# Chunk attention's probabilities turned by VectorE and GpSimd's transfers instead of TensorE

## The chip, the core and the metric

The kernel runs on one core of one Trainium2 chip. A core has engines that run side by side, each through its own instructions in order: TensorE (PE in the profile; PEld is its loading of weights) multiplies matrices and writes PSUM, VectorE (DVE) and ScalarE (ACT) work on elements, GpSimd (POOL) here fills small buffers and issues some transfers, SyncE (SP) issues nearly all transfers (DMAs). All transfers run on the core's 16 DMA engines. Engines wait for one another by semaphores. SBUF is the on-chip memory of 128 partitions, PSUM the accumulators, device memory (DRAM) holds inputs and outputs.

The metric is the device time of one execution in microseconds (us). Three runs of the kernel before took 925.45, 925.61 and 925.86 us.

## What is computed

Two layers of one mixer each, for 256 positions of width 2048. One input projection feeds three groups of heads: A, softmax attention in chunks of 64 (8 heads of 128); B, gated linear attention (4 heads); M, cross-attention into 256 memory tokens (4 heads). Each group's output is gated by a SiLU path, the groups are joined, mapped by an output projection, added to the input and normalized. Group A is where the change lies. Cut to it:

```python
def chunk_band_attention(q, k, v, rel_table):
    ...
    scores = jnp.einsum('bnqhd,bnkhd->bhnqk', qc, k_band).astype(jnp.float32) * (Dh ** -0.5)
    ...
    bias = rel_table[:, rel_idx].astype(jnp.float32)
    scores = jnp.where(valid[None, :, None, None, :], scores + bias[None, None], NEG_INF)
    p = jax.nn.softmax(scores, axis=-1).astype(v.dtype)
    out = jnp.einsum('bhnqk,bnkhd->bnqhd', p, v_band)
    return out.reshape(B, S, H, Dh)

def hybrid_layer(x, mem, w_in, rel_table, gate_w, gate_b, gla_norm_g, w_mem_kv, w_out, ln_g, ln_b):
    h = x @ w_in
    ...
    y = jnp.concatenate([y_a * jax.nn.silu(a_z), y_b * jax.nn.silu(b_z), y_m * jax.nn.silu(m_z)], axis=-1)
    out = y @ w_out
    return layer_norm(DEEPNORM_ALPHA * x + out, ln_g, ln_b)
```

With 256 positions and a band of nine chunks, a position sees its own chunk and all before it.

## The kernel before

**Weights.** Every projection is computed from pieces of weights, mostly of 512 KB, each read once. SP loads a piece into a raw buffer (`piece`, L128); ScalarE casts it to the high half (L116), VectorE subtracts to get the low half (L117), and TensorE multiplies with both halves. The pool `wp` has four buffers each for raw, high and low. `ws_half` (L240) and `as_group` (L272) run one output group, piece by piece, and call `tick` after each piece: with a share of 1 after a piece of 512 columns, of 388/512 after one of 388 columns.

**Work between the pieces.** The heads are written as generators. `tick` (L52) advances a counter by the share and runs one step of one generator that is due; a `yield n` puts off the generator's next step until the counter is n further. At most two generators are active at a time; the others wait in a list. `finish` calls `tick` until given generators are done. So a head's matmuls stand between the matmuls of two pieces in TensorE's order.

**Order.** TensorE and SP run in program order (`manual_schedule`, L49). The instructions of VectorE, ScalarE and GpSimd are put in order by a planner that simulates the program; on the chip each engine then keeps that order. Weight loads stand in SP's order where the pieces stand in the program, and SP runs ahead of TensorE as far as buffers are free.

**A head of group A** (`a_head`, L503, 8 per layer). It issues the bias load of head h + 2 on SP (`load_bias`, L820; the loads of heads 0 and 1 stand ahead of all), multiplies queries and keys into PSUM (scores for two tiles of 128 queries: 128 and 256 keys, 384 columns), adds the bias on VectorE (L511), takes the maximum (L516), the exponential and its sum on ScalarE (L518), and normalizes (L519, L521). Three steps of the counter later TensorE transposes the probabilities in three blocks of 128x128 into PSUM (L526) and ScalarE copies them to SBUF (L528); two steps later TensorE multiplies them with the values (L532, L533) and ScalarE copies the result out (L534). The bias tiles have four buffers, used in turn.

**Around it.** Per layer the generators run in this order: `gla` (group B, L311) from the third group of values on, heads 0 to 3 once the second group of keys is done (after piece 24, counted from that group of values), heads 4 to 7 after piece 48, then four heads of group M (`m_head`). The group of values has eight pieces of 388 columns; the groups of queries, keys and gates have eight pieces of 512 KB or the like. Scratch tiles come from a pool of eight buffers used in turn (`scratch`, L98), PSUM banks from one of four (`bank`, L95).

Of the kernel before, what the change touches and what calls it, by code (L numbers as in the profile page):

```python
# [8 lines left out]
F32 = mybir.dt.float32  # L9
# [4 lines left out]
ALU = mybir.AluOpType  # L14
# [4 lines left out]
P = 128  # L19
# [3 lines left out]
CH = 64  # L23
# [13 lines left out]
def hybrid_trunk_kernel(  # L37
# [7 lines left out]
    pe, dve, act, pool, sp = nc.tensor, nc.vector, nc.scalar, nc.gpsimd, nc.sync  # L45
# [4 lines left out]
    waiting, active, done, now = [], [], set(), [0]  # L50

    def tick(share=1.0):  # L52

        now[0] += share
        while True:
            while waiting and len(active) < 2:
                active.append((waiting.pop(0), 0))
            due = [e for e in active if e[1] <= now[0]]
            if not due:
                return  # L60
            active.remove(due[0])
            g = due[0][0]
            after = next(g, None)
            if after is not None:
                active.append((g, now[0] + after))
                return
            done.add(g)

    def finish(gens):
        while not all(g in done for g in gens):  # L70
            tick()

    def enter(name, bufs=1, **kw):
        return ctx.enter_context(tc.tile_pool(name=name, bufs=bufs, **kw))

    cst = enter("cst")
    per = enter("per")
    opp = enter("opp", 5)
    wp = enter("wp", 4)
    hd = enter("hd", 1)  # L80
    sc = enter("sc", 8)
    sm = enter("sm", 1)
    psd = enter("psd", 2, space=bass.MemoryType.PSUM)
    psa = enter("psa", 4, space=bass.MemoryType.PSUM)

    uid = [0]

    def nm(s):
        uid[0] += 1
        return f"{s}_{uid[0]}"  # L90

    def mm(o, l, r, start, stop):
        pe.matmul(o, l, r, start=start, stop=stop, skip_group_check=True)  # L93

    def bank():  # L95
        return psa.tile([P, 512], F32, name=nm("bk"), tag="bk")

    def scratch(shape, dtype=F32):  # L98
        return sc.tile(shape, dtype, name=nm("sc"), tag="sc")

    def small(shape, tag, bufs=1):
        return sm.tile(shape, F32, name=nm(tag), tag=tag, bufs=bufs)

    ident = cst.tile([P, P], F32, name="ident")
    lmask = cst.tile([P, 6, CH], U8, name="lmask")
    eye = cst.tile([P, CH], F32, name="eye")
    eps = cst.tile([P, 2], F32, name="eps")

    def operand():
# [130 lines left out]
    def ws_half(src, xq):  # L240

        acc = psd.tile([P, 2, 2, T], F32, name=nm("acc"), tag="acc")
        for pc in range(4):
            wh, wl = piece(src[pc], 256, 4)
            xh, _, both = xq[pc]
            for j in range(4):
                for b in range(2):
                    mm(acc[:, b].rearrange("p h t -> p (h t)"), wh[:, j, b * P:(b + 1) * P], both[:, j], pc == j == 0, False)
                for b in range(2):
                    mm(acc[:, b, 1], wl[:, j, b * P:(b + 1) * P], xh[:, j], False, pc == j == 3)  # L250
            tick()
        return acc
# [58 lines left out]
    def gla(gw, gb, ng, gq, gk, lr, asv, yraw):  # L311
# [15 lines left out]

        def keep(lev, pb):

            for par in range(2):  # L330
                pv = pb[par].rearrange("p (g c) -> p g c", c=CH)
                if lev < 0:
                    dve.tensor_tensor(pairs[par], pv, eye.unsqueeze(1).to_broadcast([P, 4, CH]), op=ALU.mult)
                else:
                    dve.copy_predicated(pairs[par], lmask[:, lev].unsqueeze(1).to_broadcast([P, 4, CH]), pv)


        pt = bank()
# [51 lines left out]
        pt = bank()  # L390
# [8 lines left out]
        for c in range(3):  # L399
            rs = slice((c % 2) * 64, (c % 2) * 64 + 64)  # L400
            t = c // 2
            for b in range(2):
                for par in range(2):
                    h = 2 * b + par
# [9 lines left out]
        for c in range(3):  # L414
            t = c // 2
            src = kv[c % 2].rearrange("p (g c) -> p g c", c=P)[:, t * 2:t * 2 + 2]
            if c == 0:
                dve.tensor_copy(st[:, 0], src)
            else:
                for b in range(2):  # L420
                    dve.scalar_tensor_tensor(st[:, c, b], st[:, c - 1, b], elast[:, b * 4 + c:b * 4 + c + 1],
                                             src[:, b], op0=ALU.mult, op1=ALU.add)
        keep(-1, diagonal)
        keep(0, first)

        for levels in ((1, 2, 3), (4, 5)):
            nxt = [decayed(LEVELS[lev]) for lev in levels]
            yield 6
            pb = [[bank() for _ in range(2)] for _ in levels[::2]]
            halves = [[p[:, i % 2 * 256:i % 2 * 256 + 256] for p in pb[i // 2]] for i in range(len(levels))]  # L430
            for kq, half in zip(nxt, halves):
                products(*kq, half)
            for lev, half in zip(levels, halves):
                keep(lev, half)
# [7 lines left out]
        po = [bank() for _ in range(2)]  # L442
        far = [bank() for _ in range(2)]
        at = [slice(i * CH, (i + 1) * CH) for i in range(2)]
        for t in range(2):
            for b in range(2):
                g = t * 2 + b
                for half in range(2):
                    for par in range(2):
                        h = 2 * b + par  # L450
                        mm(po[half][at[par], g * P:(g + 1) * P], pairs[par][at[half], g],
                           asv[at[half], t, 16 + h * P:16 + (h + 1) * P], g == 0, False)
        for odd, even in ((1, 2), (3, None)):
            for b in range(2):
                for c in (odd, even):
                    if c is not None:
                        for par in range(2):
                            g = (c // 2) * 2 + b
# [28 lines left out]
    def gla_turned(yraw, ng, y):  # L487

        for par in range(2):
# [8 lines left out]
            dve.scalar_tensor_tensor(lo, ptv, ng[:, 0:1], hi.bitcast(F32), op0=ALU.mult, op1=ALU.subtract)  # L498
            yield 1

    SCALE = P ** -0.5

    def a_head(h, load_bias, bias, q, k, asv, y):  # L503

        if h + 2 < 8:
            load_bias(h + 2)
        pb = bank()
        mm(pb[:, 0:128], q[:, 0:128], k[:, 0:128], True, True)
        mm(pb[:, 128:384], q[:, 128:256], k, True, True)
        s = scratch([P, 384])  # L510
        dve.scalar_tensor_tensor(s, pb[:, :384], SCALE, bias[h], op0=ALU.mult, op1=ALU.add)  # L511
        mx = small([P, 2], "mx", 4)
        zs = small([P, 2], "zs", 4)
        own = (slice(0, 128), slice(128, 384))
        for t in range(2):
            dve.tensor_reduce(mx[:, t:t + 1], s[:, own[t]], AX.X, ALU.max, negate=True)  # L516
        for t in range(2):
            act.activation(s[:, own[t]], s[:, own[t]], AF.Exp, bias=mx[:, t:t + 1], accum_out=zs[:, t:t + 1])  # L518
        dve.reciprocal(zs, zs)  # L519
        for t in range(2):  # L520
            dve.tensor_scalar(s[:, own[t]], s[:, own[t]], zs[:, t:t + 1], None, op0=ALU.mult)  # L521
        yield 3

        pt = bank()
        for i in range(3):
            pe.transpose(pt[:, i * P:(i + 1) * P], s[:, i * P:(i + 1) * P], ident)  # L526
        pT = scratch([P, 384])
        act.copy(pT, pt[:, :384])  # L528
        yield 2
        po = bank()  # L530
        v0 = 528 + h * P
        mm(po[:, 0:256], asv[:, 0, v0:v0 + P], pT[:, 0:256], True, False)  # L532
        mm(po[:, 128:256], asv[:, 1, v0:v0 + P], pT[:, 256:384], False, True)  # L533
        act.copy(y, po[:, :256])  # L534
        yield 2

    def m_head(h, q, mk, mv, y):
# [11 lines left out]
        dve.tensor_reduce(mx, pb.rearrange("p (t m) -> p t m", t=2), AX.X, ALU.max, negate=True)  # L549
        dve.tensor_scalar(mx, mx, SCALE, None, op0=ALU.mult)  # L550
        s = scratch([P, 2, 256])
        for t in range(2):
            act.activation(s[:, t], pb[:, t * 256:(t + 1) * 256], AF.Exp, bias=mx[:, t:t + 1], scale=SCALE, accum_out=zs[:, t:t + 1])
        dve.reciprocal(zs, zs)
# [59 lines left out]
    def wo_pieces(l, n):  # L614

        if n < 3:
            return [w512[l, G_WO + n, pc] for pc in range(8)]
        return [[w256[l, i, pc // 2][:, pc % 2 * 512:pc % 2 * 512 + 512] for i in range(2)] for pc in range(8)]
# [141 lines left out]
    for l in range(L):  # L760
# [27 lines left out]
        if l == 0:  # L788
            sp.dma_start(ident, ident_d)
            lm = wp.tile([P, 6, CH], I32, name="lm", tag="raw")  # L790
            sp.dma_start(lm, lmask_d)
            dve.tensor_copy(lmask, lm)
            dve.tensor_tensor(eye, ident[:, :CH], ident[:, CH:], op=ALU.add)

        asv = per.tile([P, 2, 1552], F32, name=nm("asv"), tag="asv")

# [21 lines left out]
        bias = {}  # L818

        def load_bias(h):  # L820
            bias[h] = hd.tile([P, 384], F32, name=nm("bias"), tag="bias", bufs=4)
            sp.dma_start(bias[h], relw[l, h])

        load_bias(0)
        load_bias(1)
        if l > 0:
# [4 lines left out]
        for half in range(2):  # L831
            values(2 + half)
            q = heads(G_AQ0 if half == 0 else G_AQ1)
            k = heads(G_AK0 if half == 0 else G_AK1)
            gens.append([a_head(half * 4 + h, load_bias, bias, q[:, h], k[:, h], asv, yraw[1 + half][:, h]) for h in range(4)])
            waiting.extend(gens[-1])
# [36 lines left out]
        for n in range(WO_N):  # L873
            if last:
                g, b = scratch([P, 512]), scratch([P, 512])
            else:
                both = per.tile([P, 2, 512], F32, name=nm("gb"), tag=f"yr{n}")
                g, b = both[:, 0], both[:, 1]
# [3 lines left out]
            src = wo_pieces(l, n)  # L882
# [122 lines left out]
```

## Time and profile before

| | before |
|---|---|
| median of three runs | 925.61 us (925.45 to 925.86) |
| the profiled execution | 925.59 us |
| its span, first to last instruction | 923.8 us |
| TensorE busy | 916.7 us, 5500 matmuls |
| VectorE busy | 587.9 us, 812 instructions |
| ScalarE busy | 498.2 us, 714 |
| GpSimd busy | 21.8 us, 49 |
| TensorE's mean granted clock | 0.998 |
| moved by DMA | 178.85 MB, mean 194 GB/s |

How to read the rows in what follows. A row of a group of instructions reads: line of the kernel, engine, operation, output <- inputs by name, shapes, count | busy us, mean ns of one | idle us of the engine just before them <- what ended it. A row in order of time reads: start us, us, engine, line, operation, tensors, count [idle before <- releaser]. A row of waits reads: waiting engine and line <- releaser and its line: us in total, times, longest. A row of DMA issues reads: tensors, queue, count, KB each, median us from the issue to the landing. A row of stretches reads: from:to, length, then busy time and count of TensorE, weight load, VectorE, ScalarE, GpSimd, then granted clock, share of the DMA engines, GB/s. Names: `bk` is a PSUM bank, `acc` a projection's accumulator, `sc` a scratch tile, `wh` and `wl` the halves of a piece, `asv` the values, `qk` queries and keys.

### The profile page before, as it was taken

The numbers are of one execution on the slowest core, as the hardware profiler recorded it, in microseconds if no ns is written. First come the engines' busy times: TensorE is split into PE (matmuls) and PEld (weight loads), VectorE is DVE, ScalarE is ACT, GpSimd is POOL, SyncE is SP. The second block draws the span as 40 slices with busy tenths as digits, with TensorE's granted clock in tenths as the row PEclk, the third lists the DMA queues.
The fourth block names the chain that finished last, engine by engine and source line by source line (L and its number), as shares of the span: only waits on it lengthen the run. The fifth ranks groups of instructions, "written<-read, shape, count | busy, mean of one in ns | idle before, by whom it ended". The sixth has DMA issues, their size and how long they took to land.

```text
span 923.8 us, 14249 instructions
## 1 busy us (share of the span) xinstructions
PE 916.7 (99%) x5500; PEld 806.5 (87%) x5500; DVE 587.9 (64%) x812; ACT 498.2 (54%) x714; POOL 21.8 (2%) x49
## 2 busy tenths in 40 slices
PE   9999999999999999999999999999999999999997
PEld 7889998998888888888888899889888888888885
DVE  6764478665564666555587666975655555766566
ACT  6644485484454675433566445754744555754350
POOL 1000000000000000000000000000000000110000
PEclk9999999999999999999999999999999999999999
DMA  9955865546554566756675466546555544667652
GB/s 306 334 189 174 306 207 173 161 165 194 183 162 160 171 206 200 219 193 196 227 249 164 150 205 204 193 154 196 170 193 166 164 152 160 199 222 223 198 163 92
DMA packets 71253, 178.85 MB, mean 194 GB/s; under 512 B 7304, under 2 KB 31240, under 8 KB 70928
## 3 DMA queue, kind: packets, MB, share of 16 engines
q1 hardware_dynamic: 69120, 173.30, 57.1%
q0 software_dynamic: 1920, 4.36, 1.8%
q8 instruction: 43, 0.70, 0.3%
q10 hardware_dynamic: 144, 0.26, 0.1%
q14 instruction: 26, 0.21, 0.1%
HBM read 175.77 MB, written 2.10 MB: 193 GB/s over the span
## 4 chain that ended last, share of the span: by engine, by line
PE 98%; DMA 0%; DVE 0%; ACT 0%; SPq 0%; issue 0%
PE acc L93 89%; PE bk L93 8%; PE bk L526 1%; DMA raw<-w 0%; PE bk L561 0%; PE bk L590 0%; PE bk L494 0%; PE bk L393 0%; SPq L177 0%; ACT res L746 0%; ACT wh L116 0%; DVE stats L731 0%; PE bk L340 0%; DVE res L730 0%; DVE res L682 0%
## 5 line engine op out<-in xcount | busy, mean ns | idle before, releaser
L117 DVE TENSOR_TENSOR wl<-raw,wh 128x1024 fp32r<-128x1024 f32 (+3 forms) x321 | 370.0, 1154 | 255.9 <-ACT wh L116 254.9
L116 ACT CAST wh<-raw 128x1024 fp32r<-128x1024 f32 (+3 forms) x321 | 318.7, 994 | 329.9 <-PE acc L93 236.5
L93 PE MATMUL acc<-x,wh 128*128 128x512 f32 x1248 | 398.0, 400 | 0.1
L93 PE MATMUL acc<-wh,x 128*128 128x512 f32 (+2 forms) x1236 | 357.3, 370 | 0.1
L93 PEld LDWEIGHTS acc<-x,wl 128*128 128x128 f32 x1248 | 234.4, 188 | 55.3
L93 PEld LDWEIGHTS acc<-wh,x 128*128 128x128 f32 x1236 | 227.0, 188 | 27.9 <-ACT wh L116 0.6
L93 PE MATMUL acc<-x,wl 128*128 128x256 f32 x1248 | 246.0, 278 | 0.0
L93 PE MATMUL acc<-wl,x 128*128 128x512 f32 (+2 forms) x618 | 228.0, 369 | 0.0
L93 PEld LDWEIGHTS acc<-x,wh 128*128 128x128 f32 x1248 | 192.0, 189 | 1.9 <-ACT wh L116 0.4
L93 PEld LDWEIGHTS acc<-wl,x 128*128 128x128 f32 x618 | 116.0, 188 | 15.0 <-DVE wl L117 0.9
L518 ACT ACTIVATE sc<-sc,mx 128x128 f32<-128x128 f32 (+1 forms) x32 | 14.4, 450 | 20.3 <-DVE mx L516 20.3
L511 DVE SCALAR_TENSOR_TENSOR sc<-bk,bias 128x384 f32<-128x384 f32 x16 | 8.9, 554 | 12.7 <-PE bk L93 12.7
L382 ACT ACTIVATE sc<-sc 128x512 f32<-128x512 f32 x12 | 7.6, 633 | 12.5 <-DVE sc L380 12.5
L117 DVE TENSOR_TENSOR x<-sc,x 128x512 fp32r<-128x512 f32 x20 | 13.3, 684 | 0.7 <-ACT x L116 0.7
L116 ACT CAST x<-raw 128x1024 fp32r<-128x1024 f32 x5 | 5.3, 1053 | 15.3 <-DMA raw<-memT 12.7
L117 DVE TENSOR_TENSOR x<-res,x 128x512 fp32r<-128x512 f32 (+2 forms) x14 | 10.5, 765 | 4.2 <-ACT x L116 4.1
L93 PE MATMUL bk<-qk,qk 128*128 128x128 f32 (+1 forms) x64 | 13.1, 326 | 0.0
L117 DVE TENSOR_TENSOR x<-raw,x 128x1024 fp32r<-128x1024 f32 x5 | 6.1, 1225 | 10.9 <-ACT x L116 10.9
L93 PE MATMUL bk<-sc,asv 128*128 128x256 f32 (+1 forms) x64 | 13.0, 326 | 0.0
L262 DVE SCALAR_TENSOR_TENSOR sc<-acc,sc 128x512 f32<-128x512 f32 x19 | 12.9, 681 | 0.0
L116 ACT CAST x<-sc 128x512 fp32r<-128x512 f32 x20 | 11.8, 615 | 1.3 <-DVE sc L598 1.3
L623 DVE SCALAR_TENSOR_TENSOR res<-res,acc 128x512 f32<-128x512 f32 x15 | 9.7, 684 | 4.2 <-PE acc L93 4.2
(209 smaller groups left out, 567.8 us busy)
## 6 DMA issues: line engine op xcount, KB each, us to landing
raw<-w SPq DMA_DIRECT2D x214, 512.0 KB, 3.9
raw<-w SPq DMA_DIRECT2D x64, 388.0 KB, 3.3
raw<-w SPq DMA_DIRECT2D x83, 256.0 KB, 3.2
bias<-relw SPq DMA_DIRECT2D x16, 192.0 KB, 4.1
res<-xT SPq DMA_DIRECT2D x4, 512.0 KB, 5.0
res<-xn SPq DMA_DIRECT2D x1, 2048.0 KB, 8.2
raw<-memT SPq DMA_DIRECT2D x4, 512.0 KB, 4.3
res<-memT SPq DMA_DIRECT2D x6, 256.0 KB, 6.1
```

What stands on the lines that cost most here:

```text
L93: pe.matmul(o, l, r, start=start, stop=stop, skip_group_check=True)
L116: act.copy(hi, src)
L117: dve.tensor_tensor(lo, src, hi.bitcast(F32), op=ALU.subtract)
L262: dve.scalar_tensor_tensor(dst, a, scale, dst, op0=ALU.mult, op1=ALU.add)
L382: act.activation(dd, dd, AF.Abs)
L511: dve.scalar_tensor_tensor(s, pb[:, :384], SCALE, bias[h], op0=ALU.mult, op1=ALU.add)
L518: act.activation(s[:, own[t]], s[:, own[t]], AF.Exp, bias=mx[:, t:t + 1], accum_out=zs[:, t:t + 1])
L526: pe.transpose(pt[:, i * P:(i + 1) * P], s[:, i * P:(i + 1) * P], ident)
L623: dve.scalar_tensor_tensor(r, r, ALPHA, acc, op0=ALU.mult, op1=ALU.add)
```

## The change

The three transposes on TensorE and the copy by ScalarE leave the head. In their place `turned` lets VectorE transpose the probabilities in blocks of 32x32 into a scratch tile, GpSimd issue four transfers of 32 partitions each into a tile in device memory (each writes 128 rows of 96 floats), and GpSimd issue one transfer that reads that tile back into `pT`, 128 partitions of 384 floats. `pT` and the tile in device memory have three buffers each of their own. The two yields of 3 and 2 between scores and values become one of 7. Three generators may be active instead of two. The bias tiles have three buffers instead of four. The tile `eye` is no longer kept: each layer makes it in a scratch tile.

```diff
-            while waiting and len(active) < 2:
+            while waiting and len(active) < 3:
                 active.append((waiting.pop(0), 0))
...
+    tp = enter("tp", 3)
...
+    drm = enter("drm", 3, space=bass.MemoryType.DRAM)
...
-    eye = cst.tile([P, CH], F32, name="eye")
...
         def keep(lev, pb):
 
+            if lev < 0:
+                eye = scratch([P, CH])
+                dve.tensor_tensor(eye, ident[:, :CH], ident[:, CH:], op=ALU.add)
...
+    def turned(dst, src, n):
+
+        blocks = scratch([P, 4, n])
+        dve.transpose(blocks.rearrange("p b (g j) -> p g b j", j=32), src.rearrange("p (g b j) -> p g b j", b=4, j=32))
+        home = drm.tile([P, 4, n], F32, name=nm("home"), tag=f"home{n}")
+        for a in range(4):
+            pool.dma_start(home[:, a].rearrange("(b i) n -> i b n", b=4), blocks[a * 32:(a + 1) * 32])
+        pool.dma_start(dst, home)
...
             dve.tensor_scalar(s[:, own[t]], s[:, own[t]], zs[:, t:t + 1], None, op0=ALU.mult)
-        yield 3
-
-        pt = bank()
-        for i in range(3):
-            pe.transpose(pt[:, i * P:(i + 1) * P], s[:, i * P:(i + 1) * P], ident)
-        pT = scratch([P, 384])
-        act.copy(pT, pt[:, :384])
-        yield 2
+        pT = tp.tile([P, 4, 96], F32, name=nm("pT"), tag="pT")
+        turned(pT, s, 96)
+        yield 7
         po = bank()
         v0 = 528 + h * P
-        mm(po[:, 0:256], asv[:, 0, v0:v0 + P], pT[:, 0:256], True, False)
-        mm(po[:, 128:256], asv[:, 1, v0:v0 + P], pT[:, 256:384], False, True)
+        pv, pov = pT.rearrange("p a (g j) -> p g a j", j=32), po[:, :256].rearrange("p (t a j) -> p t a j", t=2, j=32)
+        mm(pov, asv[:, 0, v0:v0 + P], pv[:, 0:2], True, False)
+        mm(pov[:, 1], asv[:, 1, v0:v0 + P], pv[:, 2], False, True)
         act.copy(y, po[:, :256])
...
-            dve.tensor_tensor(eye, ident[:, :CH], ident[:, CH:], op=ALU.add)
...
         def load_bias(h):
-            bias[h] = hd.tile([P, 384], F32, name=nm("bias"), tag="bias", bufs=4)
+            bias[h] = hd.tile([P, 384], F32, name=nm("bias"), tag="bias", bufs=3)
             sp.dma_start(bias[h], relw[l, h])
```

## The prediction

> **What bounds the kernel now.** I read the page from the top, then the waits of TensorE and of the DMA queue on SP, then the instructions in order of time around the heads of chunk attention.
>
> ```profile
> span 923.8 us, 14249 instructions
> PE 916.7 (99%) x5500; PEld 806.5 (87%) x5500; DVE 587.9 (64%) x812; ACT 498.2 (54%) x714; POOL 21.8 (2%) x49
> PE 98%; DMA 0%; DVE 0%; ACT 0%; SPq 0%; issue 0%
> ...
> PE bk L93 <- DVE eps L759: 1.1, 1, 1.1
> ```
>
> TensorE is busy 99% of the span, it is 98% of the chain that ended last, and its longest wait is 1.1 us, at the start. So any work taken from TensorE shortens the run, and any moment in which it lacks an operand lengthens it. The profiled execution took 925.59 us: 923.8 of span and 1.8 around it; the median of the runs is 925.61. I work from 925.6.
>
> What keeps TensorE fed is SP, whose queue is in program order and runs ahead:
>
> ```profile
> SPq L141 <- DVE wl L117: 516.3, 232, 5.4
> SPq L822 <- DVE sc L511: 5.0, 2, 2.8
> ...
> 198.34 0.56 DVE L511 SCALAR_TENSOR_TENSOR sc<-bk,bias 128x384 f32<-128x384 f32 x1 [1.98 <-PE bk L93]
> 198.93 0.33 SPq L822 DMA_DIRECT2D bias<-relw  x1
> ...
> 229.28 0.43 SPq L822 DMA_DIRECT2D bias<-relw  x1
> ```
>
> SP normally waits for a raw buffer (L141 on the subtraction L117). Twice it waited at L822, the load of a head's bias, for L511, which reads an older bias: L511 ended at 198.34 + 0.56 = 198.90 and the load left at 198.93. With four bias buffers that cost 2.8 us of lead at most. The load at 229.28 stands in the code just after head 5 starts, and head 5's score product ran at 250.49 (next fence): SP leads TensorE by 21 us.
>
> **The change, part by part.** First the prices of TensorE's pieces of work:
>
> ```profile
> 174.85 0.82 PE L93 MATMUL bk<-qk,qk 128*128 128x128 f32 x4
> 177.71 1.16 PE L93 MATMUL bk<-sc,sc 64*64 64x64 f32 x64
> 185.26 0.49 PE L526 MATMUL bk<-ident,sc 128*128 128x128 f32 x3
> ...
> 235.25 0.81 PE L93 MATMUL bk<-sc,asv 128*128 128x256 f32 x4
> 247.05 0.82 PE L93 MATMUL bk<-qk,qk 128*128 128x128 f32 x4
> 250.49 0.82 PE L93 MATMUL bk<-qk,qk 128*128 128x128 f32 x4
> 256.72 0.49 PE L526 MATMUL bk<-ident,sc 128*128 128x128 f32 x3
> 259.87 0.49 PE L526 MATMUL bk<-ident,sc 128*128 128x128 f32 x3
> 263.00 0.81 PE L93 MATMUL bk<-sc,asv 128*128 128x256 f32 x4
> 266.45 0.81 PE L93 MATMUL bk<-sc,asv 128*128 128x256 f32 x4
> ```
>
> These are heads 4 and 5 of layer 0 (and head 0 above); between two neighbours lies one weight piece, two where the code has two. With p a piece, q the scores, t the transposes, v the values: p+q = 3.44, 2p+q = 6.23, p+t = 3.15, p+v = 3.45, so p = 2.79, q = 0.65, t = 0.36, v = 0.66; check: 235.25 to 247.05 is 4p+v = 11.8. A piece of 388 columns is 177.71 - 174.85 - q = 2.21, and the recurrence's step at 177.71 costs 185.26 - 177.71 - 3 x 2.21 = 0.92.
>
> (1) *Transposes removed from TensorE.* The row of the group is 48 matmuls; their price by spacing is t per head, between 0.24 (only the three starts) and 0.36. I take 0.34: 16 x 0.34 = **-5.4 us**. The value products keep their sizes and stay at v.
>
> (2) *Order of steps.* With three active and yields of 7 and 2, I followed the counter of `tick` by hand. The same count for the kernel before gives the order seen in the trace (head 0 after piece 25, counted from the third group of values, heads 4 and 5 after 49 and 50). After the change: scores of heads 0 to 7 after pieces 25, 27, 33, 37, 49, 50, 51, 59; values after 34, 36, 40, 44, 56, 57, 58, 66. No `finish` has to idle.
>
> (3) *Three bias buffers.* Now the load for head h+2 waits for head h-1's L511, and head h may start one piece after head h-1. Load 7 (in head 5, after piece 50) needs head 4's L511 (after piece 49); load 3 (after 27) needs head 0's (after 25). SP, 21 us ahead, stops there, with every later weight piece behind it. Prices:
>
> ```profile
> L511 DVE SCALAR_TENSOR_TENSOR sc<-bk,bias 128x384 f32<-128x384 f32 x16 | 8.9, 554 | 12.7 <-PE bk L93 12.7
> L117 DVE TENSOR_TENSOR wl<-raw,wh 128x1024 fp32r<-128x1024 f32 x248 | 302.5, 1222 | 192.8 <-ACT wh L116 192.3
> L116 ACT CAST wh<-raw 128x1024 fp32r<-128x1024 f32 x248 | 259.6, 1049 | 244.6 <-PE acc L93 161.8 <-issue 68.2 <-DMA raw<-w 4.7
> L117 DVE TENSOR_TENSOR wl<-raw,wh 128x776 fp32r<-128x776 f32 x64 | 61.8, 966 | 60.1 <-ACT wh L116 59.9
> L116 ACT CAST wh<-raw 128x776 fp32r<-128x776 f32 x64 | 53.9, 843 | 82.3 <-PE acc L93 74.7 <-issue 4.0 <-DMA raw<-w 3.4
> ...
> raw<-w SPq DMA_DIRECT2D x214, 512.0 KB, 3.9
> raw<-w SPq DMA_DIRECT2D x64, 388.0 KB, 3.3
> raw<-w SPq DMA_DIRECT2D x2, 128.0 KB, 2.8
> ```
>
> At load 7, from the start of head 4's scores: L511 ends at 0.86 + 0.56 = 1.42 (its row at 247.91, below), the bias issue takes 0.43, then piece 51 leaves at 1.88, lands 3.9 later, is cast in 1.05 and subtracted in 1.22: high half at 6.9, low half at 8.15 with 0.05 per handover. TensorE gets to piece 51 at q + p + q = 4.09. It waits 2.8, does two matmuls (0.47), then waits 0.8 for the low half: 3.6, and 0.3 more as half a reduction of another head may stand ahead on VectorE: 3.9. Bounds: a landing of 2.8 (the 128 KB row) gives 2.8; a whole subtraction ahead gives 5.1. Two layers: **+7.8 us**.
>
> At load 3: high half at 1.88 + 3.3 + 0.05 + 0.84 = 6.1, low half at 7.1; TensorE arrives at q + 2.21 + 0.92 + 2.21 + q = 6.64 and needs the low half at about 7.0. 0 to 1.2 us, taken 0.5: two layers **+1.0 us**. Loads 4 and 5 find four to six pieces between, over 11 us, and hold nobody. After each hold SP refills four raw buffers at once.
>
> (4) *The turn itself.* It replaces a PSUM copy on ScalarE by a VectorE transpose and five transfers of GpSimd, and must end within the time to the values.
>
> ```profile
> 247.91 0.56 DVE L511 SCALAR_TENSOR_TENSOR sc<-bk,bias 128x384 f32<-128x384 f32 x1 [0.77 <-PE bk L93]
> 251.05 0.55 DVE L521 TENSOR_SCALAR sc<-sc,zs 128x128 f32<-128x128 f32 x2
> 256.36 0.55 DVE L521 TENSOR_SCALAR sc<-sc,zs 128x128 f32<-128x128 f32 x2
> ...
> L360 DVE TENSOR_TENSOR_SCAN b<-sc,sc 128x512 f32<-128x512 f32 x2 | 2.4, 1224 | 0.2
> L879 POOL DMA_DIRECT2D gb<-ln_g x4 | 2.2, 542 | 180.7 <-PE bk L494 129.1 <-DVE sc L863 51.6
> ...
> gb<-ln_g POOLq DMA_DIRECT2D x4, 256.0 KB, 5.7
> gb<-ln_b POOLq DMA_DIRECT2D x4, 256.0 KB, 6.3
> gwraw<-gate_w POOLq DMA_DIRECT2D x6, 16.0 KB, 3.4
> gbrow<-gbrow POOLq DMA_DIRECT2D x4, 8.0 KB, 1.7
> ng<-norm_g POOLq DMA_DIRECT2D x2, 0.5 KB, 4.6
> bias<-relw SPq DMA_DIRECT2D x16, 192.0 KB, 4.1
> ```
>
> Normalized probabilities: 4.55 us after the scores begin for a first head (247.05 to 251.60), 6.4 for a second (250.49 to 256.91). No row shows a VectorE transpose: 128x384 elements cost 0.55 at L511's rate, 0.92 at the scan's (1224 x 384/512); I take 0.55 plus 0.6 of waiting: ready at 5.7 or 7.6. The four writes of 48 KB take 4 x 0.54 = 2.2 on GpSimd; the last lands between 1.7 (8 KB row) and 6.3 us later, taken 4.0, between the 3.4 of `gate_w` and the 4.6 of `norm_g`, which like these has 128 short rows. The read waits for that on GpSimd's queue, and the next head's writes stand behind it: 2.2 + 4.0 + 0.54 = 6.7 us per head. The read of 192 KB lands in 4.1 (bias) to 6.3, taken 4.9.
>
> The time that is there, from scores to values: heads 4, 5, 6: 7p and q or v three times, 21.5, and 3.9 more for 4 and 5, which the hold of (3) delays; head 3: 7p + q + v = 20.8; head 2: 22.1; others more. Heads 2, 3, 7 alone need 5.7 + 6.7 + 4.9 = 17.3. From head 4's scores: head 4 lands at 17.3 of 25.4; head 5 is ready at 11.0, finds GpSimd free at 12.4, lands at 24.0 of 28.8; head 6 (scores at 10.8) is ready at 18.4, finds GpSimd free at 19.1, lands at 30.7 of 32.3. All in time, head 6 by 1.6: **0 us**. With every unknown at its upper row (0.92, a subtraction of 1.22 ahead, 6.3 and 6.3) head 3 is late by 1.2, head 5 by 2.2, head 6 by another 5.5: 8.9 per layer, +17.8.
>
> [...]
>
> (5) *Off the path:* 16 x 0.55 = 8.8 us of VectorE in 587.9, as much off ScalarE, 80 x 0.54 = 43 us of GpSimd in 21.8, `eye` made once per layer. They are covered by TensorE's pieces; if the refill after a hold meets them, that is inside the bounds of (3).
>
> **Sum:** 925.6 - 5.4 + 7.8 + 1.0 + 0 = **929.0 us**.
>
> **The rivals.** *A. The transfers come late.* If writes and read land like `ln_g` (5.7), GpSimd needs 8.4 per head: head 5 lands at 14.1 + 14.1 = 28.2 of 28.8, head 6 at 22.5 + 14.1 = 36.6 of 32.3: 4.3 per layer, 8.6 in all, **937.6 us**. For it: weights share the DMA engines, and head 6's slack is small. Against: those rows carry five times the bytes of one write.
>
> *B. SP is not held* (the other side). If load 7 gets its buffer without stopping the weights, (3) vanishes and -5.4 stands: **920.2 us**. It decides from the point where both holds together cost under 2.7 per layer. For it: TensorE never waited where L822 did. Against: those waits took 2.8 of a lead of 21, and now the reader is one piece away.
>
> *C. TensorE comes back slow after the hold.* It would idle 2.8 and 0.8 us around 0.47 of work. The only slow stretch before is the start:
>
> ```profile
> 1.05 2.93 PE L93 MATMUL bk<-zeros 128*128 128x128 f32 x12 [1.05 <-DVE eps L759]
> ...
> 0.00:4.00 4.00, 2.93 (x12) 2.63 (x12) 0.53 (x4) 2.04 (x3) 2.93 (x10) 1.00 0.42 110
> ```
>
> There 128 columns take 2.93 / 12 = 0.24 us, against q / 6 = 0.11 for the 768 columns of the scores. One piece at that pace costs (0.24 / 0.11 - 1) x 2.79 = 3.3 more at each load 7: 929.0 + 6.6 = **935.6 us**. Against: the granted clock is 1.00 there too, so it may not be the clock, and no wait above 1.1 us tells what follows one.
> [...]
>
> **How the numbers follow.** Forecast 0.52, A 0.27, B 0.13, C 0.08. The forecast's own range is 926 (both holds at their lower bound, 925.6 - 5.4 + 5.6) to 933. The whole range reaches to 922 towards B and to 947 for A with all rows at the upper end (929.0 + 17.8). About 0.2% (1.9 us) can be told from no change. Faster: most of B, 0.10. Within: the rest of B and the forecast's low end, 0.12. Slower: 0.78.
>
> **What would show it.** Right: no L526 in the groups; in SP's waits, L822 on L511 with single waits near 18 us; TensorE idle 3 to 4 us after head 5's scores in each layer, released by the cast and the subtraction of a weight piece; no TensorE wait on the turned tile. Wrong: TensorE waits for transfers from GpSimd (A), the waits at L822 stay short (B), or the granted clock drops after the hold (C). The sum is wrong if a transpose on VectorE takes over 1.2 us or an issue on GpSimd over 0.6.

## The result and the profile after

The changed kernel takes 932.17 us (median of five, 929.49 to 934.92) against 925.86 (925.45 to 926.12) for the kernel before on the same chip: ratio 1.0072, 95% interval 1.0061 to 1.0083. The forecast was 929.0 in a range of 922 to 947. The five executions lie 5.4 us apart, those of the kernel before 0.7; the profile shown is that of the fastest, 929.49 us with a span of 927.5.

The page of the changed kernel, rows that answer to those of before:

```profile
span 927.5 us, 14308 instructions
PE 913.6 (99%) x5452; PEld 801.1 (86%) x5452; DVE 596.5 (64%) x829; ACT 487.0 (53%) x694; POOL 65.6 (7%) x129
DMA packets 74324, 185.13 MB, mean 200 GB/s; under 512 B 8584, under 2 KB 32520, under 8 KB 74000
q0 software_dynamic: 4992, 10.66, 4.1%
PE 95%; DMA 2%; DVE 1%; ACT 1%; issue 0%; SPq 0%; ACTq 0%
home<-sc POOLq DMA_DIRECT2D x64, 48.0 KB, 4.1
pT<-home POOLq DMA_DIRECT2D x16, 192.0 KB, 4.0
```

The 48 transposes are gone from TensorE (5500 to 5452 matmuls), GpSimd has its 80 new transfers, and the chain that ended last, 98% TensorE's before, now runs for 2% of the span over the landing of weights (`DMA raw<-w` on the page). First TensorE's waits, then those of SP's queue at the bias load (now L830), all of the changed kernel:

```profile
PE acc L95 <- ACT wh L117: 5.2, 2, 2.6
PE acc L95 <- DVE wl L118: 1.8, 4, 0.5
...
SPq L830 <- DVE mx L529: 72.4, 4, 19.3
SPq L830 <- DVE sc L524: 20.1, 4, 8.5
```

TensorE now waits for halves of weight pieces, twice for the cast and four times for the subtraction, and never for the turned tile. SP stands at the bias load for 92 us, up to 19.3 at a time, where it stood 5.0 in all. The row with L529, the maximum, names the instruction that stands next to the release; the reader of the bias is L524 just before it. The next rows are in order of time, heads 4 and 5 of layer 0 in the changed kernel:

```profile
246.51 0.82 PE L95 MATMUL bk<-qk,qk 128*128 128x128 f32 x4
246.98 0.81 PE L95 MATMUL acc<-x,wh 128*128 128x512 f32 x2
247.37 0.56 DVE L524 SCALAR_TENSOR_TENSOR sc<-bk,bias 128x384 f32<-128x384 f32 x1 [2.12 <-PE bk L95]
247.95 0.33 SPq L830 DMA_DIRECT2D bias<-relw  x1
248.37 1.81 SPq L142 DMA_DIRECT2D raw<-w  x4
249.95 0.82 PE L95 MATMUL bk<-qk,qk 128*128 128x128 f32 x4
252.26 1.04 ACT L117 CAST wh<-raw 128x1024 fp32r<-128x1024 f32 x1 [3.00 <-DMA raw<-w]
253.34 1.23 DVE L118 TENSOR_TENSOR wl<-raw,wh 128x1024 fp32r<-128x1024 f32 x1 [1.33 <-ACT wh L117]
253.36 0.73 PE L95 MATMUL acc<-x,wh 128*128 128x512 f32 x2 [2.59 <-ACT wh L117]
254.62 0.50 PE L95 MATMUL acc<-x,wl 128*128 128x256 f32 x2 [0.53 <-DVE wl L118]
```

Head 4's bias is read from 247.37 to 247.93, load 7 leaves at 247.95, and only then do four weight loads leave, one behind the other. Head 5's scores begin at 249.95; the piece behind them should start 0.47 later, as it does after head 4's (246.51 to 246.98), so at 250.42. It starts at 253.36: 2.94 late. The low half is due at 253.83 and used at 254.62: 0.79 more. So the hold costs 3.73 us. (The rows list 2.59 and 0.53, since a row of matmuls runs past the start of the next: 246.51 + 0.82 = 247.33, against 246.98.) Layer 1 has the same rows at 710.77 and 712.03.

### The profile page after: what moved, and what is told of

It reads as the page before. It is cut to its first block, busy times and chain, and to the rows that moved or that the text cites. A ratio compares the mean times of both kernels' runs of the same rounds, so it can differ in the third digit from the quotient of the medians.

```text
span 927.5 us, 14308 instructions
## 1 busy us (share of the span) xinstructions
PE 913.6 (99%) x5452; PEld 801.1 (86%) x5452; DVE 596.5 (64%) x829; ACT 487.0 (53%) x694; POOL 65.6 (7%) x129
## 2 busy tenths in 40 slices
DMA packets 74324, 185.13 MB, mean 200 GB/s; under 512 B 8584, under 2 KB 32520, under 8 KB 74000
## 3 DMA queue, kind: packets, MB, share of 16 engines
q0 software_dynamic: 4992, 10.66, 4.1%
## 4 chain that ended last, share of the span: by engine, by line
PE 95%; DMA 2%; DVE 1%; ACT 1%; issue 0%; SPq 0%; ACTq 0%
PE acc L95 87%; PE bk L95 7%; DMA raw<-w 2%; DVE wl L118 0%; ACT wh L117 0%; PE bk L599 0%; PE bk L570 0%; DVE sc L524 0%; PE bk L498 0%; DVE mx L529 0%; PE bk L397 0%; SPq L142 0%; ACT res L755 0%; DVE stats L740 0%; PE bk L344 0%
## 5 line engine op out<-in xcount | busy, mean ns | idle before, releaser
L511 POOL DMA_DIRECT2D home<-sc x64 | 34.9, 552 | 319.1 <-DVE sc L508 318.9
L263 DVE SCALAR_TENSOR_TENSOR qk<-acc,qk 128x512 f32<-128x512 f32 x16 | 11.0, 685 | 11.9 <-ACT qk L262 11.9
L262 ACT ACTIVATE qk<-acc 128x512 f32<-128x512 f32 x16 | 9.5, 591 | 13.8 <-PE acc L95 13.8
L524 DVE SCALAR_TENSOR_TENSOR sc<-bk,bias 128x384 f32<-128x384 f32 x16 | 8.9, 554 | 11.4 <-PE bk L95 11.0
L95 PE MATMUL bk<-pT,asv 128*128 128x256 f32 (+1 forms) x64 | 13.0, 325 | 0.0
```

Of the source, the lines that this page charges most:

```text
L262: act.mul(dst, b, scale)
L263: dve.scalar_tensor_tensor(dst, a, scale, dst, op0=ALU.mult, op1=ALU.add)
L511: pool.dma_start(home[:, a].rearrange("(b i) n -> i b n", b=4), blocks[a * 32:(a + 1) * 32])
```

## Experiments

Two theories. H: the three bias buffers, with heads that start one piece apart, hold SP's queue; the weights come late; and in the idle stretch TensorE's clock falls in some executions (the fastest of the five has a granted clock of 0.999, the others 0.992 to 0.994). T: the turn through device memory costs the time and scatters it. Every edit below was timed beside the kernel before on one chip.

**Four buffers.**

```diff
 (the changed kernel)
-            bias[h] = hd.tile([P, 384], F32, name=nm("bias"), tag="bias", bufs=3)
+            bias[h] = hd.tile([P, 384], F32, name=nm("bias"), tag="bias", bufs=4)
```

> The changed kernel with four bias buffers instead of three, all else the same. Theory H (the three bias buffers hold SP's queue at load 7 and load 3 of each layer; the hold starves TensorE for 4.4 us per layer and lets its clock drop in some executions): SP's waits at the bias load are under 3 us, TensorE waits for no weight piece in the head stages, granted clock 0.998 in every run, 920.5 to 921.5 us with a spread under 1 us. Rival T (the turn itself costs the time: GpSimd's transfers through device memory delay weights or the values, with a spread from device memory): 928 to 933 us, spread of several us stays.

Measured: 921.38 us (920.93 to 922.17) against 926.12, ratio 0.9948 (0.9936 to 0.9961), clock 0.997 to 0.999. SP waits at no bias load any more, and TensorE's longest wait for a weight piece is 0.4. The turn is still there, with the same order of instructions on TensorE, SP and GpSimd (VectorE and ScalarE are ordered a little differently). So all of the loss, and the scatter, came with the buffer that was taken away; T falls.

**Three buffers, and nothing else, in the kernel before.**

```diff
 (the kernel before)
-            bias[h] = hd.tile([P, 384], F32, name=nm("bias"), tag="bias", bufs=4)
+            bias[h] = hd.tile([P, 384], F32, name=nm("bias"), tag="bias", bufs=3)
```

> The kernel before with three bias buffers instead of four, transposes on TensorE, two generators active. By the counter, heads 1 and 2 and heads 4 and 5 start one piece apart, so load 4 and load 7 of each layer wait for a reader one piece ahead. Theory H: four holds of 3.7 us, so 940 to 941 us, and 2 to 6 us more where the clock drops behind them (granted clock 0.985 to 0.995), spread over 2 us. Rival T: no transfers of GpSimd here, so no spread and no clock below 0.998; and if the buffers cost nothing, 926 us.

Measured: 950.59 us (949.12 to 951.97), ratio 1.0263 (1.0249 to 1.0278), clock 0.987 to 0.989. The hold is shown without the turn's transfers. The size was missed: 3.6 us above the upper end of what was expected (947). Rows in order of time, heads 1 and 2 of layer 0, then stretches of 4 us (the last three figures are the granted clock, the share of the DMA engines and GB/s):

```profile
198.07 0.82 PE L93 MATMUL bk<-qk,qk 128*128 128x128 f32 x4
200.59 0.56 DVE L511 SCALAR_TENSOR_TENSOR sc<-bk,bias 128x384 f32<-128x384 f32 x1
201.17 0.33 SPq L822 DMA_DIRECT2D bias<-relw  x1
207.04 1.22 PE L93 MATMUL acc<-x,wh 128*128 128x512 f32 x2 [4.71 <-ACT wh L116]
...
202.00:206.00 4.00, 0.32 (x2) 0.00 (x0) 1.79 (x6) 0.54 (x3) 0.00 (x0) 1.00 0.90 288
206.00:210.00 4.00, 2.92 (x8) 2.01 (x9) 2.95 (x6) 3.95 (x8) 0.00 (x0) 0.51 0.84 311
210.00:214.00 4.00, 4.00 (x17) 3.44 (x17) 2.71 (x4) 1.90 (x2) 0.00 (x0) 0.63 0.89 276
```

VectorE was occupied and read the bias only at 200.59, 2.5 us after the scores began instead of 0.86, so this hold lasts 4.71. Then the clock stands at 0.51 and 0.63 where it had been 1.00: the two matmuls at 207.04 take 1.22 us together, against 0.73 after the hold in the changed kernel's fastest run. Over the whole run the four holds make TensorE wait 4.7, 3.1, 4.0 and 2.7 us for a high half and twice 0.5 for a low one, and the clock stands at 0.50 for 20.5 us in four stretches that begin at the end of a hold or just behind it. The waits and half of the 20.5 come to 25.8 us; the span is 26.4 longer than that of the kernel before. The half is an estimate from the clock of 0.50; by the rows it is a little less, 0.45: pairs of matmuls with a high half start 1.28 us apart behind the hold (208.90 and 210.18) and 0.70 ahead of it (199.41 and 200.11).

**The bias loaded later.**

```diff
 (the changed kernel, still three buffers)
-        if h + 2 < 8:
-            load_bias(h + 2)
...
         yield 7
+        if h + 3 < 8:
+            load_bias(h + 3)
...
         load_bias(1)
+        load_bias(2)
```

> The changed kernel with three bias buffers, but head h loads the bias of head h+3 at its second step, seven units of the counter after it read its own; the first three loads stand ahead. Theory H: it is the place of the load behind a late reader, not the number of buffers: 920.5 to 922 us, clock 0.998, SP's waits at the bias load a few us at most and none of TensorE for weights. Rival (three buffers are too few in any place): 925 us or more.

Measured: 920.79 us (919.91 to 921.71), ratio 0.9941 (0.9929 to 0.9954), clock 0.997 to 0.998. SP waits 10.5 us at these loads, 2.2 at most, and TensorE waits for no weights there. So it is the distance between the load and the last reader of its buffer, not the count of buffers. This version and the one with four buffers beat both kernels.

**Three active generators alone.**

```diff
 (the kernel before)
-            while waiting and len(active) < 2:
+            while waiting and len(active) < 3:
```

> The kernel before with three active generators instead of two; transposes on TensorE, four bias buffers. Theory H: the order alone is worth nothing, 925.5 to 926.5 us, so that the gain of e1_four_bias is that of the transposes taken from TensorE (5 us; 16 heads at 0.3 us). Rival (the gain is that of the earlier heads, or of fewer PSUM banks in use): 921 to 923 us.

Measured: 925.91 us (925.11 to 926.88), ratio 0.9999 (0.9991 to 1.0008). Three active generators are worth nothing by themselves. So the 4.7 us between the kernel before and the one with four buffers (926.12 - 921.38), and the 5.3 with the later load, are put down to the transposes taken from TensorE: 0.30 to 0.33 us per head. That is what is left over, not a run of its own; it fits that the 48 transposes are the only matmuls gone and that TensorE waits for next to nothing in either kernel (1.7 us in all before, 2.3 with four buffers).

**The changed kernel again, unaltered,** for an execution with a low clock.

> The changed kernel once more, unaltered, for the executions in which the granted clock is low. Theory H with the clock: runs fall into two kinds, 929.5 us at clock 0.998 or more and 932 to 935 us at 0.992 to 0.994; if the profiled one is of the second kind, its clock is below 1.00 only in the few us after the hold at load 7 (250 to 262 us, 708 to 720 us), and its waits for weights are the same 3.7 us. Rival (transfers differ from run to run): in a slow run the waits for weights or for the turned tile are longer and the clock is unchanged where TensorE works.

Measured: 933.06 us (930.0 to 934.46, six executions). Five have a clock of 0.992 to 0.995 and take 932.18 to 934.46; one has 0.999 and takes 930.0. With the first five, nine of eleven executions are of the low kind, 933.3 on the mean, and two of the other, 929.7. The profiled one is low (932.18, span 930.2). Its stretches around the holds of both layers, cut where the clock changes in the trace and 3.41 us before each fall, then one more stretch and the wait of layer 1:

```profile
250.00:253.41 3.41, 1.07 (x6) 0.46 (x4) 2.15 (x5) 1.60 (x4) 2.17 (x4) 1.00 0.99 358
253.41:256.82 3.41, 2.95 (x9) 2.34 (x9) 2.93 (x6) 2.42 (x4) 0.00 (x0) 0.50 1.01 386
...
707.38:710.79 3.41, 1.40 (x9) 0.91 (x7) 2.39 (x7) 0.77 (x1) 1.82 (x4) 1.00 1.02 366
710.79:717.62 6.83, 6.46 (x19) 5.12 (x20) 5.89 (x8) 5.26 (x9) 2.96 (x6) 0.50 0.98 337
...
712.00:716.00 4.00, 3.96 (x13) 3.14 (x13) 3.77 (x7) 2.85 (x3) 1.00 (x2) 0.50 0.98 355
...
711.12 1.22 PE L95 MATMUL acc<-x,wh 128*128 128x512 f32 x2 [2.35 <-ACT wh L117]
```

The fastest run of the changed kernel, around its holds and in the same stretch of layer 1:

```profile
248.95:252.37 3.42, 1.82 (x12) 1.28 (x10) 2.46 (x7) 0.42 (x3) 1.41 (x3) 1.00 0.87 307
252.37:255.78 3.41, 1.89 (x9) 1.37 (x10) 2.03 (x5) 2.88 (x6) 0.76 (x2) 1.00 1.02 368
...
712.00:716.00 4.00, 3.97 (x23) 3.57 (x24) 3.54 (x7) 2.91 (x3) 1.16 (x3) 1.00 0.96 339
```

The wait is not longer (2.35), but behind it the clock stands at 0.50, for 3.41 us in layer 0 and 6.83 us in layer 1, and in 712 to 716 TensorE starts 13 matmuls instead of 23 at a clock of 1.00. Half of these 10.24 us, by the same estimate, is 5.1 us; some of it falls in the wait itself or stands where the low half would have been waited for, and the span is 2.7 us longer than the fast run's.

The traces of the two also differ in where the hold falls. In both, and in that of the kernel before, the moments at which the record of the clock begins or changes lie whole multiples of 3.41 us from one another: in the low run the fall at 253.41, the rise at 256.82, the next fall 453.97 later (133 of them) and the rise 6.83 after that; in the kernel before and in the fastest run of the changed one the first and the last, 914.77 and 918.19 apart (268 and 269). In the low run the hold falls inside one such interval (in layer 1 all but its last 0.33 us), in which TensorE is busy for only 1.07 or 1.40 us, and the clock falls at its end. In the fastest run, counted on from the beginning of its record at 6.61, it lies in layer 0 across the border of two (252.37), TensorE is busy 1.82 and 1.89 us in them, and the clock stays at 1.00. The four falls in the kernel before with three buffers follow intervals with 0.00 to 0.88 us of work. So the kind may depend on where the hold falls in these intervals. That is read from two traces of the eleven executions; no run tests it.

The transfers do not differ in the way T had it: TensorE waits 5.1 us for high halves and 1.2 for low ones in the low run, 5.2 and 1.8 in the fastest, and for the turned tile in neither.

**The idle stretch filled,** twice.

```diff
 (the changed kernel, after head 5's scores)
         mm(pb[:, 128:384], q[:, 128:256], k, True, True)
+        if h == 5:
+            for _ in range(22):
+                mm(pb[:, 384:512], ident, ident, True, True)
```

> The changed kernel with 22 idle matmuls of 128x128 after head 5's scores, which add no result: they keep TensorE busy for about 2.4 us of the hold at load 7. Theory H with the clock: nothing is saved in the hold, so the fastest run stays near 929.5 us, but the clock does not drop: granted clock 0.998 or more in every run, median 929 to 930.5 us, spread under 1 us. Rival (the spread comes from the transfers or from device memory, and the low granted clock is its sign only): median stays 931 to 933 us with a spread of 4 us or more.

Measured: 933.25 us (932.75 to 934.44), clock 0.997 to 0.999 in all five. The clock behaved as H says, the time did not: each of the 22 ran as two instructions,

```profile
251.10 5.08 PE L95 MATMUL bk<-ident 128*128 128x128 f32 x44
255.93 0.70 PE L95 MATMUL acc<-x,wh 128*128 128x512 f32 x2
```

so the filling lasted 4.83 us (251.10 to 255.93) in a hold of 3.73, 2.2 too much in two layers, which makes 931.7 of 929.5; another 1.5 of the median stays unexplained. The same with `range(12)`:

> As e4_filled with 12 idle matmuls instead of 22: each ran as two instructions of 0.11 us, so 22 filled 4.84 us, 1.1 us more than the hold, in each layer. Twelve fill 2.6 of 3.7 us. Theory H with the clock: fastest run near 929.5, median 929 to 931 us, granted clock 0.997 or more in all runs. Rival (the low clock has nothing to do with the idle stretch): median 932 us, clock 0.992 to 0.994 in most runs.

Measured: 932.35 us (930.96 to 933.86), clock 0.997 to 0.999 in all six. Again the clock held, in eleven filled executions of eleven, against two of eleven unfilled; again the time is not that of the fast kind. TensorE's waits name the reason:

```profile
221.86 0.89 PE L95 MATMUL bk<-pT,asv 128*128 128x256 f32 x4 [0.49 <-DMA pT<-home]
736.09 0.92 PE L95 MATMUL bk<-pT,asv 128*128 128x256 f32 x4 [1.72 <-DMA pT<-home]
```

The planner, which sees the filling, ordered GpSimd, VectorE and ScalarE otherwise, and the turned tile came late for two heads. So the filled kernels show that the clock falls for want of work; what that costs in time they do not show. That rests on the stretches above.

**Less time for the turn.**

```diff
 (the changed kernel with four bias buffers)
-        yield 7
+        yield 5
```

> As e1_four_bias with a yield of 5 instead of 7 between the scores and the values, so two weight pieces (5.6 us) less time for the turn: 15.9 us for heads 4 to 6. From the rows of the changed kernel a turn ends 17 to 18 us after its scores begin. Theory H (the transfers are just hidden at 7): TensorE waits 1 to 3 us for the turned tile at several heads, 924 to 931 us, and the granted clock may fall. Rival (the transfers end much earlier than their rows say, or are not waited for): 921 us, no wait.

Measured: 938.45 us (937.14 to 938.6), ratio 1.0131 (1.0118 to 1.0145), clock 0.991 to 0.993; 17 us above the yield of 7. TensorE's wait, the stretch of layer 0's heads, and one of TensorE's rows in it:

```profile
PE bk L95 <- DMA pT<-home: 12.1, 6, 4.7
...
200.00:300.00 100.00, 94.39 (x511) 81.38 (x510) 59.02 (x97) 47.22 (x80) 16.43 (x30) 0.97 0.60 185
...
219.19 1.62 PE L95 MATMUL bk<-pT,asv 128*128 128x256 f32 x4 [4.62 <-DMA pT<-home]
```

The sign is H's, the size is not: 938.45 us, where 931 was the most expected; 12.1 us of waits, worst at head 2 of each layer (4.6 and 4.7), and the clock falls here too (0.97 over 200 to 300 us). The 17 to 18 us that the expectation gave a turn were too few: in the changed kernel's profile head 2's takes 21.8 (see (4) below). So at 7 the turn is hidden, but two pieces less expose it.

## Why the prediction was right, and where it was off

**(1) Transposes.** Predicted -5.4; the runs give -4.7 (four buffers) and -5.3 (later load), with three active generators shown to be worth nothing.

**(2) Order.** As counted: heads 4 and 5 one piece apart, and no `finish` idles.

**(3) The hold.** Load 7 was priced at 3.9 and measured 3.73, by the steps named: the reader at 1.42 after head 4's scores began (1.42 measured, 247.93 - 246.51), the first half at 6.9 (6.85), the low half at 8.15 (8.11). Two small parts were off and partly made up for each other: the 0.3 for a reduction standing ahead on VectorE did not come (the subtraction at 253.34 starts 0.04 after the cast ends), and TensorE was ready at 3.91 (250.42 - 246.51) instead of 4.09. Load 3 was priced at 0.5:

```profile
183.86 0.62 PE L95 MATMUL acc<-wh,x 128*128 128x388 f32 x2
184.86 0.44 PE L95 MATMUL acc<-wl,x 128*128 128x388 f32 x1 [0.38 <-DVE wl L118]
```

With 0.18 from one start to the next, the low half was due at 184.22: 0.64. Both layers: 2 x (3.73 + 0.64) = 8.7, predicted 8.8. With 5 us saved that is +3.7, which is what the fastest run's span shows (927.5 - 923.8).

**(4) The turn.** Hidden, as forecast, and near its prices: transpose 0.58 (0.55), writes 4.1 (4.0), read 4.0 (4.9). Rows of VectorE's transposes and of GpSimd in order of time:

```profile
L508 DVE STREAM_TRANSPOSE sc<-sc x16: 567/578/580, 178.3 to 744.4; 128x384 f32<-128x384 f32 x16
...
250.96 2.18 POOL L511 DMA_DIRECT2D home<-sc  x4 [26.63 <-DVE sc L508]
257.61 2.17 POOL L511 DMA_DIRECT2D home<-sc  x4 [4.48 <-DVE sc L508]
259.77 0.56 POOL L512 DMA_DIRECT2D pT<-home  x1
...
271.48 0.56 POOL L512 DMA_DIRECT2D pT<-home  x1 [3.76 <-DMA home<-sc]
```

One step was wrong here without harm: I had the next head's writes stand behind a head's read. The planner put head 5's writes (257.61) ahead of head 4's read (259.77), which so waited for head 5's transpose. Head 6's read leaves at 271.48 and lands about 275.5, and its values run at 278.47: 3.0 us to spare, not 1.6.

The head with the least to spare was another one, head 2, for which 17.3 of 22.1 us were counted. ScalarE and VectorE in order of time, then GpSimd and TensorE:

```profile
204.28 1.28 ACT L531 ACT_TABLE_LOAD   x1
208.47 0.57 DVE L508 STREAM_TRANSPOSE sc<-sc 128x384 f32<-128x384 f32 x1
...
215.22 0.56 POOL L512 DMA_DIRECT2D pT<-home  x1 [3.70 <-DMA home<-sc]
...
220.11 0.81 PE L95 MATMUL bk<-pT,asv 128*128 128x256 f32 x4
```

Its scores began at 197.98, but casts, subtractions and group B's normalization stood ahead on ScalarE and VectorE, with two loads of a function table of 1.28 us each on ScalarE (202.67 before a square root, 204.28 before the exponential), so that the transpose was done 11.1 us after the scores began, not 5.7. The tile landed at 219.79, 21.8 us after them, with 0.3 to spare. That the turn was hidden there was in part luck.

**Rival A** did not come true at a yield of 7, and does at 5. The writes landed in 4.1 us and the read in 4.0 (medians), where A counted 5.7 for each.

**Rival B** fell: SP was held.

**Rival C is the step that failed.** The forecast took an idle stretch of 2.8 and 0.8 us as harmless and gave the slow return 0.08. It happened in nine of eleven executions, and so sets the median: 929.0 was the fast kind (929.5 and 930.0), 932.17 is the low one. Its price, 6.6, was too high: the low kind is 3.5 us above the other (933.3 - 929.7). In the profiled low run the clock was halved for 3.4 and 6.8 us, and part of the 5.1 us that this takes would have been waited out anyway. That 932.17 still lies in the forecast's own range of 926 to 933 is luck: no term of the sum stood for the clock. The profile's 1.00 at the start, held against C, was no evidence: the trace's record of the clock begins only at 4.64 us, and a stretch without a record shows as 1.00 (0.00 to 4.00). That a stretch of 2.8 us leaves the clock alone was my assumption, and no run had shown it: behind listed waits of 2.34 and 2.35 the clock fell to 0.50.

## What to carry to other kernels

Where one queue issues loads in program order, a buffer that is short by one holds not only its own load but everything behind it (here four weight loads, and 3.73 us of TensorE's time): ask where the last reader stands, and how far the queue runs ahead. A load can be moved behind its reader as well as given another buffer. When TensorE is the bound, price an idle stretch like these (waits of 2.3 to 4.7 us) at what it lasts and, from these runs, 1.8 to 2.6 us more for the clock behind it (3.5 us over two holds between the two kinds of the changed kernel, half of 20.5 over four in the kernel before with three buffers), and expect executions to scatter as these do (929.5 to 934.9).

## What was not expected of the hardware

The writes' 384-byte rows did not travel as small packets. GpSimd's queue shows 4992 - 1920 = 3072 more packets. By the trace's list of packets, 1280 of them are of 4 B (16 for each of the 80 transfers; they are the 8584 - 7304 under 512 B on the pages), 1280 of 3072 B and 512 of 4608 B; none is of 384 B. This comes out if a write of 48 KB is 16 packets of 3072 B, eight rows each, and a read of 192 KB is 16 of 3072 B and 32 of 4608 B. And three 128x128 transposes in a dense stream of matmuls cost TensorE only 0.30 to 0.33 us in all, where the row of a single one says 0.27 in the kernel before.
